# A decoder block on one core: 24 sets of weight sums instead of 20, four FFN blocks with five by-seven steps, and seven by-seven steps in the second half of the down product

## The chip, the cores and the metric

The kernel runs on one core of one Trainium2 chip, in one launch. The metric is the device time of one execution in microseconds (us). Three runs of the kernel before took 1697.29, 1697.33 and 1697.82 us (median 1697.33). The profile comes from one more execution with the hardware profiler on, which took 1698.13 us.

## The reference, cut to what matters

One layer of a hybrid decoder: normalisation, one wide projection, dilated window attention and a gated linear recurrence, a gated merge, the mixing product, and a SwiGLU feed-forward (FFN) part. There are 256 positions, the model width is 2048, and the FFN width is 5632.

```python
a = rmsnorm(h, norm_mix_pre)
q_a, k_a, v_a, q_r, f_r, i_r, g_r, gate_a, gate_r = split_columns(a @ w_in)
...
y = sigmoid(gate_a) * (attn @ w_attn_branch) + sigmoid(gate_r) * (r_out @ w_hgrn_branch)
h = h + rmsnorm(y @ w_mix_out, norm_mix_post)

a = rmsnorm(h, norm_ffn_pre)
gt, up = split(a @ w_ffn_gate_up, [5632])
ff = (silu(gt) * up) @ w_ffn_down
h = h + rmsnorm(ff, norm_ffn_post)
```

The change touches the two FFN products: `a @ w_ffn_gate_up` (2048 to twice 5632) and the product with `w_ffn_down` (5632 to 2048).

## The kernel before, in words

**One product in three matmuls.** Every float32 operand is split into a high and a low part. A product of a weight tile and an activation tile is then three 128x512 matmuls on TensorE (PE): high by high, high by low, low by high (`prod` in `multiply_wide`, all recorded at L138). A weight tile arrives by DMA on SyncE's queue (SP) as `raw`. ScalarE (ACT) copies it to its high part (`w`, `dh`: L418, L426, L429, L439, L442, L445), and VectorE (DVE) subtracts that to get the low part (`wl`, `dl`: L420, L427, L430, L447, L449). PE needs both.

**Wide blocks and steps.** The FFN's gate and up columns are worked in 11 blocks, each a `Wide` of 512 gate and 512 up columns. A block has 8 steps, one for each 256 rows m of the weight, and the order of the steps is written out by hand as a list of pairs (m, code). The down product is two such blocks of 22 steps. A plain step (code 0) is a 2 by 2 product of tiles done with 8 products, 24 matmuls. A "by-seven" step uses a scheme of the kind of Strassen's with 7 products, 21 matmuls. It multiplies sums of weight tiles by sums of activation tiles (`by_sums`, with `w` and `wl` of the sums) and raw tiles by others (`by_raw`, with `dh` and `dl` of the raw weights). With code 1 the sums of the weights are made on DVE when the step is prepared (`sum`, L434, L440, L441). With code 2 they were made long before and are fetched from DRAM (`s`).

**Buffers and the order of work.** While step i multiplies, step i+2 is split (`prepare`, `split_wide`). There are three buffers for `raw`, three for `w`, and four with the tag "d" that `dh` and `dl` share, so that two by-seven steps can hold theirs at once. `by_sums` comes first and `by_raw` second, but in the last by-seven step of a block, and in all of the down product, it is the other way round. Each engine works off its instructions in the order in which this program issues them.

**The list before.** In the FFN, block 0 is plain, block 1 has three by-seven steps (`GATE_UP3`), and blocks 2 to 10 have four (`GATE_UP4`). Two steps of each block 1 to 10 have code 2: 20 sets of weight sums. In the down product the first half has by-seven steps at m = 4, 7, 10, 13, 16, 19, the second at m = 3, 6, 9, 12, 15, 18. For each of these, `prep_act` makes the sums of its activations on DVE (`seven_sums`, L522 to L529) and keeps them in `a7`.

**Weight sums ahead of time.** `weight_sums` is a generator that runs in the background of the 176 narrow items ("chunks") between the wide blocks, in which attention and recurrence are worked too. After each chunk `ahead_of_time` moves it on by one `yield`, unless `hold` is set. For a set it starts two loads of 512 KB into the single buffer `pre` (on SP), lets four items pass, issues two subtractions on DVE (L309, L310), an item later two more (L312, L313), and an item later the store of 1 MB to DRAM (`presum`, on ACT's queue, L316). That is seven items a set. In the same stretch a chunk's weight is split by ACT (L364) and DVE (L365) ahead of the chunk's matmuls, two chunks ahead.

The sums of the activations for the FFN's by-seven steps (`h7`) are made in `pair_sums` out of `hT`, one set for each m, and live in slots of 1024 columns (`rslot`).

Of the kernel before, what the change touches and what calls it, by code (L numbers as in the profile page):

```python
# [24 lines left out]
FF = 5632  # L25
# [17 lines left out]
]  # L43
GATE_UP3 = [(3, 0), (4, 0), (0, 2), (5, 0), (1, 1), (6, 0), (2, 2), (7, 0)]
GATE_UP4 = [(4, 0), (5, 0), (0, 2), (6, 0), (1, 1), (2, 2), (3, 1), (7, 0)]
PLACE = (0, 2, 1, 3)
DOWN = [[(m, m in by7) for m in range(KF // 2)] for by7 in (range(4, 20, 3), range(3, 19, 3))]

N_F, N_RAW, N_SPLIT, AHEAD, WARM, BRIDGE = 15, 3, 3, 2, 8, 6

# [50 lines left out]
def tile_hybrid_block(ctx: ExitStack, tc: tile.TileContext, t, out):  # L101
# [13 lines left out]
    def nm(s):  # L115
        serial[0] += 1
        return f"{s}_{serial[0]}"

    def rslot(s):
        return rpool.tile([P, 1024], F32R, tag="r", bufs=16, name=nm(s))  # L120
# [10 lines left out]
    def p3(s, dtype, n, bufs, tag=None):  # L131
        return wide_pool[-1].tile([P, n], dtype, tag=tag or s, bufs=bufs, name=nm(s))
# [161 lines left out]
    def weight_sums(jobs):  # L294

        for n in jobs:
            x = fp[0].tile([P, 2048], F32, tag="pre", bufs=1, name=nm("pre"))
            b, i = steps[n][:2]
            m = b.order[i][0]
            for g in range(2):  # L300
                nc.sync.dma_start(
                    x[:, g * 1024 : (g + 1) * 1024].rearrange("p (k c) -> p k c", k=2),
                    b.w[2 * m * P : (2 * m + 2) * P, b.cols[g] : b.cols[g] + 512]
                    .rearrange("(k p) c -> p k c", p=P),
                )
            for _ in range(4):
                yield
            r = [x[:, q * 512 : (q + 1) * 512] for q in range(4)]
            nc.vector.tensor_sub(r[2], r[2], r[0])  # L309
            nc.vector.tensor_sub(r[0], r[1], r[0])  # L310
            yield
            nc.vector.tensor_add(r[1], r[1], r[2])  # L312
            nc.vector.tensor_sub(r[3], r[3], r[1])  # L313
            yield
            pre[n] = dram.tile([P, 2048], F32, name=nm("presum"))
            nc.scalar.dma_start(pre[n], x)  # L316
            yield
# [327 lines left out]
        return row[:, None, :].to_broadcast([P, n, S])  # L645

    evacs, turns, lanes, queue = deque(), deque(), [deque(), deque()], deque()
    back, hold = deque(), [False]
    ready = set()

    def advance(q):
# [586 lines left out]
    def mix_to_ffn(i):  # L1238
# [60 lines left out]
        ffn(2, 1)  # L1299
        residual_of(5, (0, 1), False)  # L1300

    def more_h(c):
        if c + 1 < KD // 2:
            transpose_in(h_t, colg[:, 16:32], hT[0], c + 1)
        if c == 3:
            mix_gain(3, 1, wides[last_mix])
            residual_of(6, (0, 1), False)
            residual_of(7, (0, 1), False)
            lanes[0].append(second_norm())
        if c == 4:  # L1310
            lanes[1].append(pair_sums(hT[0], h7, lambda: rslot("so"), range(4)))

    def second_norm():
        ss, s2 = small("ss"), small("s2")
# [86 lines left out]
    def prep_act(m, by7):  # L1401

        q = prepared[0] // 2
        prepared[0] += 1
        fetch_act(q + (m % 2 and 2))
        f = act_in[q][:, m % 2 * 2 : m % 2 * 2 + 2, :]
        x = parts_of[m] = Split("a", 2)
        x.high(0, f)
        yield
        x.low(0, f)  # L1410
        if by7:
            dst = rslot("so").rearrange("p (z n t) -> p z n t", z=2, n=4)
            high, low = seven_sums(f, dst)
            high()
            a7[m] = sums_of(dst)
            yield
            low()
# [154 lines left out]
    add_wide_block(w, (0, FF), PLAIN, lambda k: hT[0](k), None, evac_first, True, mid=more_h)  # L1572
    spare = wides[-1], 0
    for j in range(1, 11):
        add_wide_block(w, (512 * j, FF + 512 * j), GATE_UP4 if j > 1 else GATE_UP3, lambda k: hT[0](k),
                       lambda m: h7[m], evac_ffn, j % 2 == 0,
                       pre=begin_wides if j == 1 else None, turn=1)
    for j in range(2):
# [19 lines left out]
    split(1)  # L1598
    load_upto(AHEAD + N_RAW - 1)
    for i in range(len(items)):  # L1600
        kind, n, _ = items[i]
        b, c = kind[n][:2]
        wide = kind is steps
        if wide:
            now[0] = b
        if c == 0 and b.pre:
            b.pre()
        if not wide and n in items_pre:
            items_pre[n]()
        if together <= i < together + 5:  # L1610
            if i == together:
                flush(evacs)
                mix_to_ffn(i)
            continue
        if not (wide and b.mid):
            prepare(i)
        if i >= len(items) - 3:
            continue
        multiply(i)
        if b.post:  # L1620
            b.post(c)
        if wide and c == b.last7:
            gather(b)
        advance(evacs)
        if wide and c == b.turn:
            flush(evacs)
            turn_act(turns.popleft())
        for _ in range(2):
            if turns and type(turns[0]) is not list:
                advance(turns)  # L1630
        advance_lanes()
        if not wide:
            ahead_of_time()
        if c == (len(b.order) if wide else b.steps) - 1:
            evacs.append(b.evac(b if wide else b.banks))
            if wide:
                advance(evacs)
# [63 lines left out]
```

## Time and profile before

| | |
|---|---|
| median of 3 runs | 1697.33 us |
| lowest, highest | 1697.29, 1697.82 us |
| profiled execution | 1698.13 us |
| its span of instructions | 1696.3 us |
| HBM read, written | 376.92 MB, 35.13 MB |
| matmuls of the group `acc<-w,hT` (the largest of the FFN) | 472, 152.7 us busy |
| DMA for the sums' loads, stores and fetches | 40 of 512 KB, 20 of 1024 KB, 40 of 512 KB |

The span is the time from the first to the last instruction of the core in the profiled execution, and the rest of its time lies around the span. A view by windows gives each engine's busy time in a stretch; a timeline gives one row for an instruction or a run of like ones: its start, its duration, engine, line, operation with output and inputs, and in brackets how long the engine was idle before it and whom it waited for. Matmuls overlap in the rows (a 128x512 matmul has 0.39 us, and the next starts 0.23 us behind it).

### The profile page before, as it was taken

To read this page: it belongs to the slowest core of one execution; us is meant where nothing else is said; L and a number is where in the kernel's file an instruction comes from. 1 tells how busy PE (TensorE), PEld (TensorE's weight loads), DVE (VectorE), ACT (ScalarE), POOL (GpSimd) and SP (SyncE) were. 2 spreads that over 40 slices of the span, in tenths; PEclk is the share of its full clock that TensorE was granted. 3 is DMA by queue.
4 is the path that set the end of the run, shared out by engine and by line. 5 is a ranking of instruction groups with operands and counts; after the bars stand their busy time and mean duration, and the time that the engine had idled before them with its cause. 6 is when DMAs were issued, how large, how long until landed. Compare 5 with 4: busy or idle time off the path is not lost.

```text
span 1696.3 us, 21711 instructions
## 1 busy us (share of the span) xinstructions
PE 1685.2 (99%) x8260; PEld 1416.7 (84%) x8260; DVE 1436.2 (85%) x1662; ACT 914.7 (54%) x1034; POOL 3.9 (0%) x13
## 2 busy tenths in 40 slices
PE   9999999999999999999999999999999999999997
PEld 7888888888888888888888888888888888888886
DVE  6999888867998988885668888888888888898997
ACT  6655555544444434445445547555555555565663
POOL 0000000000000000000000000000000000000000
PEclk9999999999999999999999999999999999999999
DMA  8667666768677767787858646777777777777773
GB/s 285 205 224 243 230 233 228 234 222 309 225 254 252 256 223 243 253 310 275 295 172 275 210 162 227 269 250 252 254 255 253 249 248 272 257 266 256 248 244 130
DMA packets 228904, 413.48 MB, mean 244 GB/s; under 512 B 12816, under 2 KB 79552, under 8 KB 226240
## 3 DMA queue, kind: packets, MB, share of 16 engines
q1 hardware_dynamic: 218544, 373.93, 65.4%
q10 hardware_dynamic: 10192, 38.15, 6.0%
q8 instruction: 64, 1.05, 0.3%
q14 instruction: 40, 0.33, 0.1%
q0 software_dynamic: 64, 0.02, 0.0%
HBM read 376.92 MB, written 35.13 MB: 243 GB/s over the span
## 4 chain that ended last, share of the span: by engine, by line
PE 98%; DVE 1%; ACT 0%; issue 0%; DVEq 0%; ACTq 0%
PE acc L138 62%; PE aux L138 34%; PE aux L930 0%; DVE wl L420 0%; PE aux L610 0%; PE aux L1348 0%; DVE fz L1475 0%; PE acc L1348 0%; ACT w L418 0%; ACT junk L1429 0%; PE aux L597 0%; DVE e L1425 0%; PE aux L1110 0%; DVE yT L578 0%; PE aux L1220 0%
## 5 line engine op out<-in xcount | busy, mean ns | idle before, releaser
L138 PE MATMUL acc<-xT,w 128*128 128x256 f32 (+1 forms) x2048 | 366.8, 338 | 0.0
L420 DVE TENSOR_TENSOR wl<-raw,w 128x2048 fp32r<-128x2048 f32 (+1 forms) x141 | 306.6, 2182 | 68.8 <-ACT w L418 67.1
L138 PEld LDWEIGHTS acc<-xT,w 128*128 128x128 f32 x2048 | 311.9, 188 | 44.7 <-DVE w L365 0.3
L418 ACT ACTIVATE w<-raw 128x2048 fp32r<-128x2048 f32 (+1 forms) x141 | 256.3, 1827 | 109.3 <-PE acc L138 35.1
L364 ACT ACTIVATE w<-raw 128x1024 fp32r<-128x1024 f32 x176 | 185.7, 1058 | 220.5 <-PE acc L138 169.6
L365 DVE TENSOR_TENSOR w<-raw,w 128x1024 fp32r<-128x1024 f32 x176 | 214.8, 1221 | 95.9 <-ACT w L364 95.2
L138 PE MATMUL acc<-w,xT 128*128 128x512 f32 x578 | 169.1, 392 | 0.0
L439 ACT ACTIVATE w<-sum 128x1024 fp32r<-128x1024 f32 x56 | 59.5, 1063 | 177.8 <-DVE sum L434 170.6
L138 PE MATMUL acc<-w,hT 128*128 128x512 f32 x472 | 152.7, 391 | 0.4 <-DVE hT L1232 0.4
L447 DVE TENSOR_TENSOR wl<-sum,w 128x1024 fp32r<-128x1024 f32 x112 | 134.8, 1221 | 13.2 <-ACT w L439 13.2
L138 PEld LDWEIGHTS acc<-w,xT 128*128 128x128 f32 x578 | 108.1, 188 | 22.2
L138 PE MATMUL aux<-w,hT 128*128 128x512 f32 x374 | 120.0, 389 | 0.0
L449 DVE TENSOR_TENSOR dl<-raw,dh 128x1536 fp32r<-128x1536 f32 x56 | 98.3, 1756 | 14.3 <-ACT dh L445 12.2
L138 PE MATMUL aux<-w,xT 128*128 128x512 f32 x344 | 109.8, 389 | 0.0
L138 PEld LDWEIGHTS acc<-w,hT 128*128 128x128 f32 x472 | 88.5, 188 | 19.0 <-DVE hT L1232 0.8
L138 PE MATMUL acc<-wl,hT 128*128 128x512 f32 x236 | 91.9, 389 | 0.0
L445 ACT ACTIVATE dh<-raw 128x1536 fp32r<-128x1536 f32 x56 | 82.7, 1476 | 8.0 <-PE aux L138 4.4
L138 PE MATMUL acc<-w,a 128*128 128x512 f32 x268 | 83.7, 389 | 0.0
L138 PE MATMUL aux<-w,a 128*128 128x512 f32 x268 | 83.7, 389 | 0.0
L138 PEld LDWEIGHTS aux<-w,hT 128*128 128x128 f32 x374 | 70.2, 188 | 14.6
L138 PE MATMUL acc<-w,so 128*128 128x512 f32 x234 | 78.8, 391 | 0.0
L138 PEld LDWEIGHTS aux<-w,xT 128*128 128x128 f32 x344 | 64.6, 188 | 13.4
(298 smaller groups left out, 2964.3 us busy)
## 6 DMA issues: line engine op xcount, KB each, us to landing
raw<-in_w_in SPq DMA_DIRECT2D x270, 512.0 KB, 4.8
raw<-in_w_ffn_gate_up SPq DMA_DIRECT2D x156, 512.0 KB, 4.8
raw<-in_w_ffn_down SPq DMA_DIRECT2D x88, 512.0 KB, 5.4
pre<-in_w_ffn_gate_up SPq DMA_DIRECT2D x40, 512.0 KB, 6.5
presum<-pre ACTq DMA_DIRECT2D x20, 1024.0 KB, 4.7
s<-presum SPq DMA_DIRECT2D x40, 512.0 KB, 7.0
raw<-in_w_mix_out SPq DMA_DIRECT2D x32, 512.0 KB, 4.9
act<-acts SPq DMA_DIRECT2D x22, 512.0 KB, 6.5
```

The costliest lines, as they stand in the source:

```text
L138: nc.tensor.matmul(ps, lhsT, rhs, start=start, stop=stop, skip_group_check=True)
L364: nc.scalar.activation(wh, raw, AF.Copy)
L365: nc.vector.tensor_sub(wl, raw, wh.bitcast(F32))
L418: nc.scalar.activation(hi[:, c], raw[:, c], AF.Copy)
L420: nc.vector.tensor_sub(lo[:, c], raw[:, c], hi[:, c].bitcast(F32))
L439: nc.scalar.activation(hi[:, :1024], s[:, :1024], AF.Copy)
L445: nc.scalar.activation(dhi, d, AF.Copy)
L447: nc.vector.tensor_sub(lo[:, c], s[:, c], hi[:, c].bitcast(F32))
L449: nc.vector.tensor_sub(dlo, d, dhi.bitcast(F32))
```

## The change

There are four edits.

1. `GATE_UP5` is a new list with five by-seven steps, one after the other, and blocks 3, 5, 7 and 9 use it. The step m = 4, plain before, becomes a by-seven step with code 2. This makes 24 sets of weight sums instead of 20.
2. The second half of the down product has by-seven steps at m = 2, 4, 7, 10, 13, 16, 18. Those at 4, 7, 10, 13 and 16 use the activation sums that the first half made (`m not in a7`), so two sets are made in this half instead of six.
3. `weight_sums` starts the loads of a set only behind an odd item (`count[0]`), and three items pass before the first pair of subtractions instead of four. A set takes six items.
4. `pair_sums` makes a fifth set of `h7` (m = 4). Its first four slots come from the tag "so" of the wide blocks' pool, the fifth from `rslot`.

```diff
+GATE_UP5 = [(5, 0), (6, 0), (0, 2), (2, 2), (1, 1), (4, 2), (3, 1), (7, 0)]
 PLACE = (0, 2, 1, 3)
-DOWN = [[(m, m in by7) for m in range(KF // 2)] for by7 in (range(4, 20, 3), range(3, 19, 3))]
+DOWN = [[(m, m in by7) for m in range(KF // 2)] for by7 in (range(4, 20, 3), (2, 4, 7, 10, 13, 16, 18))]
...
         for n in jobs:
+            while count[0] % 2 == 0:
+                yield
             x = fp[0].tile([P, 2048], F32, tag="pre", bufs=1, name=nm("pre"))
...
-            for _ in range(4):
+            for _ in range(3):
                 yield
...
-    back, hold = deque(), [False]
+    back, hold, count = deque(), [False], [0]
...
+    def h7_slot():
+        return p3("so", F32R, 1024, 4) if len(h7) < 4 else rslot("so")
+
...
-            lanes[1].append(pair_sums(hT[0], h7, lambda: rslot("so"), range(4)))
+            lanes[1].append(pair_sums(hT[0], h7, h7_slot, range(5)))
...
-        if by7:
+        if by7 and m not in a7:
             dst = rslot("so").rearrange("p (z n t) -> p z n t", z=2, n=4)
...
-        add_wide_block(w, (512 * j, FF + 512 * j), GATE_UP4 if j > 1 else GATE_UP3, lambda k: hT[0](k),
+        order = GATE_UP3 if j == 1 else GATE_UP5 if j in (3, 5, 7, 9) else GATE_UP4
+        add_wide_block(w, (512 * j, FF + 512 * j), order, lambda k: hT[0](k),
...
-        kind, n, _ = items[i]
+        count[0], (kind, n, _) = i, items[i]
```

The lists and the pacing move instructions on DVE and ACT. Three places follow. The numbers behind the names count tiles, and the line numbers of the changed kernel are up to six higher than before.

**ACT, an FFN block with the new list (block 3), and the block in the same place before.** `L426` and `L429` make `w` and `dh` of a code 2 step, `L439`, `L442` and `L445` those of a code 1 step, `L418` is a plain step, and the rows on `act` hand over the results of the block before. Before, from the step (0,2) to (1,1):

```order
L426 ACTIVATE w_9301<-s_9227 128x1024
L426 ACTIVATE w_9301<-s_9228 128x1024
L429 ACTIVATE dh_9307<-raw_9199 128x1536
L418 ACTIVATE w_9344<-raw_9231 128x2048
L1349 ACTIVATE act_9379<-acc_9380 128x512
L1349 ACTIVATE act_9379<-acc_9386 128x512
L1353 DMA acts_9392<-act_9379 128x1024
L439 ACTIVATE w_9394<-sum_9396 128x1024
L442 ACTIVATE w_9394<-sum_9396 128x1024
L445 ACTIVATE dh_9402<-raw_9268 128x1536
```

And now, from (0,2) to (1,1):

```order
L429 ACTIVATE w_9351<-s_9273 128x1024
L429 ACTIVATE w_9351<-s_9274 128x1024
L432 ACTIVATE dh_9357<-raw_9245 128x1536
L429 ACTIVATE w_9394<-s_9314 128x1024
L429 ACTIVATE w_9394<-s_9315 128x1024
L432 ACTIVATE dh_9400<-raw_9277 128x1536
L1355 ACTIVATE act_9435<-acc_9436 128x512
L1355 ACTIVATE act_9435<-acc_9442 128x512
L1359 DMA acts_9448<-act_9435 128x1024
L442 ACTIVATE w_9450<-sum_9452 128x1024
L445 ACTIVATE w_9450<-sum_9452 128x1024
L448 ACTIVATE dh_9458<-raw_9318 128x1536
```

The plain step (6,0) between the two has given way to the code 2 step (2,2). Behind these rows follow (4,2) and (3,1), where before (2,2) and (3,1) stood, so five steps with a `dh` stand one behind the other.

**DVE, the same two places.** `L427` and `L430` make the low parts of a code 2 step, `L420` that of a plain one, `L434` begins the sums of the weights of a code 1 step, and the rows on `e` work on the results of the block before. Before:

```order
L427 TENSOR_TENSOR wl_9302<-s_9227,w_9301 128x1024
L427 TENSOR_TENSOR wl_9302<-s_9228,w_9301 128x1024
L430 TENSOR_TENSOR dl_9308<-raw_9199,dh_9307 128x1536
L1385 TENSOR_TENSOR e_9255<-e_9255,e_9257 128x512
L1385 TENSOR_TENSOR e_9256<-e_9256,e_9258 128x512
L420 TENSOR_TENSOR wl_9345<-raw_9231,w_9344 128x2048
L434 TENSOR_TENSOR sum_9396<-raw_9268 128x1024
```

And now:

```order
L430 TENSOR_TENSOR wl_9352<-s_9273,w_9351 128x1024
L430 TENSOR_TENSOR wl_9352<-s_9274,w_9351 128x1024
L433 TENSOR_TENSOR dl_9358<-raw_9245,dh_9357 128x1536
L1391 TENSOR_TENSOR e_9301<-e_9301,e_9303 128x512
L1391 TENSOR_TENSOR e_9302<-e_9302,e_9304 128x512
L430 TENSOR_TENSOR wl_9395<-s_9314,w_9394 128x1024
L430 TENSOR_TENSOR wl_9395<-s_9315,w_9394 128x1024
L433 TENSOR_TENSOR dl_9401<-raw_9277,dh_9400 128x1536
L437 TENSOR_TENSOR sum_9452<-raw_9318 128x1024
```

Where one `wl` of 2048 columns stood, two of 1024 and a `dl` of 1536 stand.

**DVE, the recurrence stretch, around chunks 75 to 77.** `w<-raw,w` are the low halves of chunks, `pre` the weight sums, the rest attention. Before:

```order
L365 TENSOR_TENSOR w_4719<-raw_4524,w_4719 128x1024
L884 TENSOR_TENSOR w_4738<-sum_4712,tabs 64x512 x2
L365 TENSOR_TENSOR w_4741<-raw_4575,w_4741 128x1024
L890 TENSOR_TENSOR sum_4712<-sum_4712,tabs 128x512
L891 TENSOR_TENSOR qk_4601<-sum_4712,w_4738 128x512
L309 TENSOR_TENSOR pre_4496<-pre_4496 128x512
L310 TENSOR_TENSOR pre_4496<-pre_4496 128x512
L365 TENSOR_TENSOR w_4770<-raw_4575,w_4770 128x1024
```

And now:

```order
L312 TENSOR_TENSOR pre_4469<-pre_4469 128x512
L313 TENSOR_TENSOR pre_4469<-pre_4469 128x512
L368 TENSOR_TENSOR w_4730<-raw_4533,w_4730 128x1024
L887 TENSOR_TENSOR w_4749<-sum_4721,tabs 64x512 x2
L315 TENSOR_TENSOR pre_4469<-pre_4469 128x512
L316 TENSOR_TENSOR pre_4469<-pre_4469 128x512
L368 TENSOR_TENSOR w_4754<-raw_4584,w_4754 128x1024
L893 TENSOR_TENSOR sum_4721<-sum_4721,tabs 128x512
L894 TENSOR_TENSOR qk_4610<-sum_4721,w_4749 128x512
L368 TENSOR_TENSOR w_4783<-raw_4584,w_4783 128x1024
```

Both pairs of a set have moved ahead of the low halves of chunks 75 and 76, and none stands ahead of chunk 77 any more.

## The prediction, made before the changed kernel ran

> **What bounds the kernel now.** I read the page first: the busy share of TensorE and the chain that ended last.
>
> ```profile
> PE 1685.2 (99%) x8260; PEld 1416.7 (84%) x8260; DVE 1436.2 (85%) x1662; ACT 914.7 (54%) x1034; POOL 3.9 (0%) x13
> ...
> PE 98%; DVE 1%; ACT 0%; issue 0%; DVEq 0%; ACTq 0%
> ```
>
> The matmuls are the time: PE is busy for 1685.2 us of the span, and 98% of the chain is PE. VectorE (DVE) comes next, and its 85% is a mean over stages. The view of PE's waits says what little PE waited for:
>
> ```profile
> PE aux L138 <- DVE warm L162: 1.2, 1, 1.2
> PE acc L138 <- DVE hT L1232: 0.4, 1, 0.4
> PE acc L138 <- DVE gate L1147: 0.2, 1, 0.2
> ```
>
> So a matmul that goes is worth its full place in PE's row, unless a new wait takes the place. The view by windows, cut where the L1348 transposes of successive FFN blocks start, prices one product (three 128x512 matmuls). The first row is a block with three by-seven steps, the second one with four. Columns: window, length, busy time of PE, PEld, DVE, ACT and POOL with counts, granted clock, DMA share, GB/s.
>
> ```profile
> 1048.05:1090.42 42.37, 42.37 (x192) 35.17 (x191) 37.85 (x38) 23.82 (x21) 0.00 (x0) 1.00 0.80 269
> 1090.42:1132.12 41.70, 41.70 (x190) 34.61 (x189) 36.70 (x33) 24.13 (x21) 0.00 (x0) 1.00 0.74 254
> ```
>
> PE is busy without a gap in both, so one product less is 42.37 − 41.70 = 0.67 us. DVE is busy for 36.70 of 41.70 us, with room on the mean only.
>
> **The change, part by part.**
>
> *Removed matmuls.* Four FFN blocks lose one product each, and the down product's second half loses one (seven by-seven steps for six): 5 × 0.67 = 3.35, with matmul starts (below) 5 × 0.68 = 3.40. I take **−3.4 us**. That is 0.20% of 1697.33, just the size below which a measurement of this kernel can't tell a change from none (3.39 us). So even the full gain is at the edge, and any wait pulls it inside.
>
> *FFN blocks 3, 5, 7, 9.* Now five by-seven steps follow one another: s2 = (0,2), s3 = (2,2), s4 = (1,1), s5 = (4,2), s6 = (3,1). Tiles dh and dl share four buffers, which is two steps' worth. So ACT may write dh of a step only when PE has left the step two places back. Before, only the third and fourth in a row had to ask ((2,2) and (3,1)), with a plain step behind. The trace shows this wait at (3,1). The first fence is PE, the second ACT, the third DVE; columns are start, duration, operation, and in brackets the idle time before and its releaser.
>
> ```profile
> 1189.20 0.39 PE L138 MATMUL aux<-dl,hT 128*128 128x512 f32 x1
> ...
> 1194.64 0.39 PE L138 MATMUL acc<-dl,hT 128*128 128x512 f32 x1
> ```
>
> ```profile
> 1176.90 1.05 ACT L442 ACTIVATE w<-sum 128x1024 fp32r<-128x1024 f32 x1
> 1177.85 1.48 ACT L445 ACTIVATE dh<-raw 128x1536 fp32r<-128x1536 f32 x1
> ...
> 1187.68 1.06 ACT L442 ACTIVATE w<-sum 128x1024 fp32r<-128x1024 f32 x1 [0.33 <-DVE sum L441]
> 1189.63 1.49 ACT L445 ACTIVATE dh<-raw 128x1536 fp32r<-128x1536 f32 x1 [0.89 <-PE aux L138]
> ```
>
> ```profile
> 1179.36 1.76 DVE L449 TENSOR_TENSOR dl<-raw,dh 128x1536 fp32r<-128x1536 f32 x1
> ...
> 1183.31 1.75 DVE L430 TENSOR_TENSOR dl<-raw,dh 128x1536 fp32r<-128x1536 f32 x1
> 1184.98 1.22 DVE L434 TENSOR_TENSOR sum<-raw 128x1024 f32<-128x1024 f32 x1
> ...
> 1191.15 1.76 DVE L449 TENSOR_TENSOR dl<-raw,dh 128x1536 fp32r<-128x1536 f32 x1 [1.16 <-ACT dh L445]
> ```
>
> The 20th of the 21 matmuls of (1,1) starts at R = 1189.20 and dh(3,1) at R + 0.43. Its dl ends at 1192.91; PE reads it at 1194.64, 24 matmuls behind R (5.44/24 = 0.2267 each), 1.73 early. In the changed blocks this chain begins one step sooner and is one step longer. From R in s3: dh(s5) at R + 0.43; dl(s5) 1.52 later (1189.63→1191.15); then on DVE's queue, behind it, the sums of s6, 1.67 later (1183.31→1184.98); ACT's second high half 2.70 behind these (1184.98→1187.68); dh(s6) 0.95 behind that (1176.90→1177.85); dl(s6) 1.51 later (1177.85→1179.36), lasting 1.76. Sum: R + 10.54. PE reads dl(s6) as the second matmul of s6, because the last by-seven step of a block takes its raw products first: one matmul left of s3, 21 of s4, 21 of s5, two of s6, so R + 45 × 0.2267 = R + 10.20. **PE waits 0.34 us.** What a short wait for DVE costs beside itself shows at the one PE has now:
>
> ```profile
> 1004.87 0.40 PE L138 MATMUL acc<-wl,hT 128*128 128x512 f32 x1
> 1005.68 0.73 PE L138 MATMUL acc<-w,hT 128*128 128x512 f32 x2 [0.41 <-DVE hT L1232]
> 1006.25 0.39 PE L138 MATMUL acc<-wl,hT 128*128 128x512 f32 x1
> ```
>
> The three steps from 1004.87 to 1006.25 take 1.38 where 0.68 is usual: 0.70 lost for 0.41 of waiting. I take about half of that surplus beside the 0.34: 0.5 us a block, four blocks, **+2.0**. Ends: 0 (the chain 0.34 shorter, 3% of its length) and 0.8 a block (3.2 in all).
>
> *More sets of weight sums (24 for 20), every six items for seven.* They run in the recurrence stretch, where DVE also makes the low half of each weight chunk (L365). A set has two pairs of subtractions, L309/L310 and L312/L313. Four sets add 8 pairs, and nearly all others move to other chunks. Where DVE idles ahead of PE a pair costs nothing; where it runs full it makes the next low half late. The worst place, by the order, is where both pairs of a set now stand ahead of the low halves that before stood at 569.26 and 571.93, with none there before. DVE first, then ACT:
>
> ```profile
> 571.93 1.23 DVE L365 TENSOR_TENSOR w<-raw,w 128x1024 fp32r<-128x1024 f32 x1
> ...
> 574.41 0.68 DVE L309 TENSOR_TENSOR pre<-pre 128x512 f32<-128x512 f32 x1
> 575.12 0.69 DVE L310 TENSOR_TENSOR pre<-pre 128x512 f32<-128x512 f32 x1
> 575.73 1.22 DVE L365 TENSOR_TENSOR w<-raw,w 128x1024 fp32r<-128x1024 f32 x1
> ...
> 614.13 1.23 DVE L365 TENSOR_TENSOR w<-raw,w 128x1024 fp32r<-128x1024 f32 x1
> ```
>
> ```profile
> 574.89 1.06 ACT L364 ACTIVATE w<-raw 128x1024 fp32r<-128x1024 f32 x1 [2.21 <-PE acc L138]
> ...
> 616.84 1.06 ACT L364 ACTIVATE w<-raw 128x1024 fp32r<-128x1024 f32 x1 [2.19 <-PE acc L138]
> ```
>
> A pair takes 575.73 − 574.41 = 1.32. DVE's rows show no idle time for 15 us ahead, so the low half of 571.93 ends at 573.16 + 2.64 = 575.80. ACT's row at 574.89, which waits for PE to leave the chunk before, is when PE wants it: 0.9 late, about 1.0 with restarting. The pairs that stood behind it (574.41 and one more) leave the next chunks, which gives back some 0.3 (chosen between 0 and 1.0). The other place is the chunk of 614.13: its low half ends at 615.36 and is wanted at 616.84, a margin of 1.48. Two pairs make it 2.64 − 1.48 = 1.16 late, of which about 0.6 is lost, as PE itself comes 0.7 later from the first place (1.0 − 0.3). At the other moved pairs I found an idle stretch or a margin. Sum **+1.3**, ends 0 and 6 (each of the four new sets giving 1.5 us).
>
> *Down product, second half.* By-seven steps are m = 2, 4, 7, …; at m = 2 and m = 4 only one plain step lies between, and raw products come first. The high and low parts of m = 4, laid end to end on DVE behind the evacuation:
>
> ```profile
> 1572.58 0.68 DVE L578 TENSOR_TENSOR a<-act,a 128x512 fp32r<-128x512 f32 x1
> ...
> 1576.30 1.22 DVE L434 TENSOR_TENSOR sum<-raw 128x1024 f32<-128x1024 f32 x1
> ...
> 1579.49 0.28 DVE L522 SCALAR_TENSOR_TENSOR s<-act 128x128 f32<-128x128 f32 x1
> ...
> 1580.42 2.35 DVE L447 TENSOR_TENSOR wl<-sum,w 128x1024 fp32r<-128x1024 f32 x2
> 1582.69 0.68 DVE L529 TENSOR_TENSOR so<-s,so 128x512 fp32r<-128x512 f32 x1
> ...
> 1584.96 0.74 DVE L1434 SCALAR_TENSOR_TENSOR fz<-e,r2c,fpost 128x512 f32<-128x512 f32 x1
> ...
> 1589.09 0.68 DVE L578 TENSOR_TENSOR a<-act,a 128x512 fp32r<-128x512 f32 x1
> ```
>
> ```profile
> 1587.82 0.39 PE L138 MATMUL aux<-dl,a 128*128 128x512 f32 x1
> ```
>
> A by-seven step's DVE work is 1584.96 − 1576.30 = 8.66; the piece from 1584.96 to 1589.09 stands for the plain step between, 4.13. The second by-seven step reuses its activation sums, so the 0.93 (1579.49→1580.42) and about 0.6 of L529 fall away: 7.13. From 1572.58: 8.66 + 4.13 + 7.13 = 1592.50. PE reads dl of before's m = 3 at 1587.82; the new m = 4 comes a by-seven step (4.76, 21 matmuls) later, 1592.58. No margin: **+0.2**, ends 0 and 0.6. Four sets of sums fewer shorten nothing else, since DVE is late nowhere else there.
>
> *At no cost:* the fifth set of hT sums falls in block 1, where DVE is busy 37.85 of 42.37 us; five fresh instructions of about 0.3 to 0.7 us would show only if that 4.5 us were gone. Each five-step block reads 768 KB more (768 KB raw and two times 512 KB of sums for 1 MB raw), 19 GB/s over 41 us; with the 254 GB/s shown this is 273, near the 269 (share 0.80) that block 1 bears without a gap.
>
> **Sum:** −3.4 + 2.0 + 1.3 + 0.2 = +0.1. The profiled execution took 1698.13 us (span 1696.3 and 1.8 around it), 0.8 above the median of the three runs; I put the difference to the median: 1697.33 + 0.1 = **1697.4**.
>
> **Rivals.**
>
> *A. The gain is whole.* DVE chains have slack that I do not see: an idle queue would start the sums of s6 before dl(s5), were they ordered so. Against it stands the order in which they are issued; for it, that all three overruns are under 1.2 us. Time 1697.33 − 3.4 = 1693.9.
>
> *B. The sums' round trip binds (slower).* A set has one buffer: load it, four subtractions, store it, and only then load the next. The page's rows of DMA issues end in the median to landing:
>
> ```profile
> pre<-in_w_ffn_gate_up SPq DMA_DIRECT2D x40, 512.0 KB, 6.5
> presum<-pre ACTq DMA_DIRECT2D x20, 1024.0 KB, 4.7
> s<-presum SPq DMA_DIRECT2D x40, 512.0 KB, 7.0
> ```
>
> ```profile
> L309 DVE TENSOR_TENSOR pre<-pre x20: 675/684/692, 366.3 to 827.6; 128x512 f32<-128x512 f32 x20
> ```
>
> ```profile
> DMA to landing us min/median/max: 3.9/6.7/8.7
> ```
>
> The first row is the view of L309, the second that of the tile `presum`, stores and loads together. From issuing the store to the next set's first pair lie the store (4.7) and the load (6.5, its second half some 0.9 behind): 12.1 us. After the change four items lie there, before five. The row of L309 gives a mean item: 19 sets of seven items in 461.3 us, 3.47 each, so 13.9 us for four and 17.3 for five. A plain item without attention or recurrence is eight matmuls of 512 columns and eight of 256, 8 × 1.5 × 0.2267 = 2.72; four of these are 10.9. Where the trip is the longer, DVE stands at L309 for a load, with low halves behind it and PE behind those. With 8.7, the longest landing, for both transfers a trip takes 17.4, which is 3.5 over 13.9; less DVE's margin of about 1.5 it costs PE 2 us. If one set in eight meets that, three sets: 1697.4 + 5.8 = 1703. It decides from trips of 13.9 + 1.5 = 15.4 us on. Against it: medians give 12.1. The Trainium skill, "DMA: Bandwidth & Descriptors", section "Latency and other measured facts", says that HBM's access time is 0.2 us on average and 2 us at high load, and that it makes most of a DMA's fixed cost. It speaks against the shorter cycle, whose two transfers each end in such an access: at two more times 2 us every trip would be 16.1, 0.7 over the 15.4, and 24 sets would give 17 us more, 1714. The trace shows 4.7 for a megabyte stored with that time already in it, so I give this nothing beyond B's chance.
>
> *C. Late in more places.* 40 moved pairs fall on chunks that I hold to have margin. If the two places are really seven, at 0.6 each, that is +3: 1700.4.
>
> **How the numbers follow.** Forecast (gain eaten by short waits, 1695.6 to 1699.5 by the bounds taken together) 0.67; A 0.18, of which 0.13 lies at or past the 0.2% bound; C 0.05; B 0.10. The range from 1693.8 to 1700.8 holds the forecast, most of C and about half of A, 0.80. Faster 0.13; slower B with half of C, 0.12; same 0.75.
>
> **What would show it.** PE's waits should gain four rows' worth of `dl` (L452 in the new numbering) of 0.3 to 0.6 us; windows of the odd blocks should be 41.0 + 0.5. The stretch around 575 and 615 should show PE waiting for the low half. If odd blocks take 41.0 without waits, my chain is wrong by its 0.34 and A holds; if the subtractions of the sums (L312 in the new numbering) sit idle for `pre`, B does. DVE idle for `pre` at many sets, or a gap in an FFN block over 1 us, would break the sum.

## The result, and the profile after

The changed kernel took 1700.83 us (median of 12 runs, 1699.95 to 1703.45), the kernel before beside it 1697.78 us (12 runs, 1697.02 to 1698.13). The ratio is 1.0019, with a 95% interval from 1.0011 to 1.0027: 0.2% slower. That is 0.03 us beyond the upper end of the range on record, 1700.8. Against the kernel before beside it the change is +3.05 us, where the prediction had +0.1. The profiled execution took 1700.86 us, with a span of 1699.1.

The page of the changed kernel answers to the two lines shown of before, and its rows of DMA issues to two of the three of the sums:

```profile
PE 1684.6 (99%) x8245; PEld 1413.2 (83%) x8245; DVE 1453.8 (86%) x1677; ACT 920.9 (54%) x1041; POOL 3.8 (0%) x13
...
PE 90%; DVE 5%; DMA 2%; ACT 1%; issue 1%; SPq 0%; DVEq 0%; ACTq 0%
...
pre<-in_w_ffn_gate_up SPq DMA_DIRECT2D x48, 512.0 KB, 5.7
presum<-pre ACTq DMA_DIRECT2D x24, 1024.0 KB, 6.4
```

PE has its 15 matmuls less, but the chain that ended last now runs for 8% of the span through DVE, DMA and ACT; before it was PE for 98%. At the median a set's store takes 1.7 us longer to land than before (6.4 for 4.7), and a load 0.8 less (5.7 for 6.5). The view of PE's waits names two new ones:

```profile
PE acc L139 <- DVE w L368: 2.1, 4, 0.8
PE aux L139 <- DVE warm L163: 1.2, 1, 1.2
PE aux L139 <- DVE dl L452: 1.0, 4, 0.3
```

`w L368` is the low half of a weight chunk in the recurrence stretch, and `dl L452` that of the step (3,1) in the four odd FFN blocks. The view of DVE's waits shows what DVE itself stood for in the stretch:

```profile
DVE pre L312 <- DMA pre<-in_w_ffn_gate_up: 10.6, 8, 2.9
...
DVE pre L312 <- issue: 3.9, 4, 2.4
```

In 12 of 24 sets DVE stood for the loads of the sums, 14.5 us in all. (Where the second row says `issue`, the pair starts about 0.1 us behind the landing of the set's second load, as it does in the first row.) Before, it was 1.9 us in all, at 3 sets. The windows of an odd and an even block (the odd one is the first row):

```profile
1135.43:1177.04 41.61, 41.35 (x186) 33.98 (x185) 37.88 (x34) 24.37 (x21) 0.00 (x0) 1.00 0.73 242
1093.74:1135.43 41.69, 41.69 (x189) 34.62 (x188) 36.76 (x34) 25.60 (x23) 0.00 (x0) 1.00 0.79 277
```

An odd block is 0.08 us shorter than an even one, where one product less is worth 0.68.

**Where the time went, by stages.** The first matmuls wait for the inputs, and differ by up to a us between executions of any kernel, so the stretch is counted from PE's 101st matmul to the first transposes of the FFN (L1348 before, L1354 after); the rest is from there to PE's last matmul. Both are differences of starts in the trace of one execution. The stretch varies from execution to execution: the runs of the changed kernel spread over 3.5 us, those of the kernel before over 1.1.

| kernel | stretch, us | against before | rest, us | against before |
|---|---|---|---|---|
| before | 1023.02 | | 638.59 | |
| after | 1026.35 | +3.33 | 637.80 | −0.79 |
| new pacing alone | 1029.64 | +6.62 | 638.62 | +0.03 |
| down product alone | 1023.07 | +0.05 | 638.16 | −0.43 |
| after, dl(4,2) later | 1026.56 | +3.54 | 635.42 | −3.17 |
| after, early store | 1025.89 | +2.87 | 637.61 | −0.98 |
| after, buffer in halves | 1030.43 | +7.41 | 637.58 | −1.01 |
| after, one load only | 1024.36 | +1.34 | 637.65 | −0.94 |
| after, tenth set later | 1024.63 | +1.61 | 637.64 | −0.95 |
| 22 sets, seven items | 1030.92 | +7.90 | 636.78 | −1.81 |
| 24 sets, fourth set later, dl(4,2) later | 1023.81 | +0.79 | 635.41 | −3.18 |
| 22 sets, last six at six items | 1029.92 | +6.90 | 636.75 | −1.84 |

So the rest, with the FFN and the down product, gave 0.8 us of the 3.4, and the stretch lost 3.3. PE's matmuls, held against those of before one by one, fall back there in steps: 0.57 at 410 (of the time before) and 0.12 right behind, 0.89 at 427, 0.92 at 575 (0.13 of it won back at 583), 0.42 at 617, 0.24 near 463, and a few of 0.1.

### The profile page after: what moved, and what is told of

It reads as the page before. It is cut to its first block, busy times and chain, and to the rows that moved or that the text cites. A ratio compares the mean times of both kernels' runs of the same rounds, so it can differ in the third digit from the quotient of the medians.

```text
span 1699.1 us, 21740 instructions
## 1 busy us (share of the span) xinstructions
PE 1684.6 (99%) x8245; PEld 1413.2 (83%) x8245; DVE 1453.8 (86%) x1677; ACT 920.9 (54%) x1041; POOL 3.8 (0%) x13
## 4 chain that ended last, share of the span: by engine, by line
PE 90%; DVE 5%; DMA 2%; ACT 1%; issue 1%; SPq 0%; DVEq 0%; ACTq 0%
PE acc L139 57%; PE aux L139 32%; DVE w L368 1%; DMA pre<-in_w_ffn_gate_up 1%; DMA presum<-pre 1%; DVE dl L452 0%; PE aux L933 0%; ACT dh L432 0%; DVE wl L423 0%; ACT dh L448 0%; PE aux L613 0%; PE aux L1354 0%; DVE fz L1481 0%; DVE sum L437 0%; PE acc L1354 0%
## 5 line engine op out<-in xcount | busy, mean ns | idle before, releaser
L423 DVE TENSOR_TENSOR wl<-raw,w 128x2048 fp32r<-128x2048 f32 (+1 forms) x136 | 295.4, 2179 | 64.5 <-ACT w L421 62.6
L421 ACT ACTIVATE w<-raw 128x2048 fp32r<-128x2048 f32 (+1 forms) x136 | 246.8, 1823 | 98.3 <-PE acc L139 31.1
L368 DVE TENSOR_TENSOR w<-raw,w 128x1024 fp32r<-128x1024 f32 x176 | 214.5, 1221 | 76.6 <-ACT w L367 74.3
L442 ACT ACTIVATE w<-sum 128x1024 fp32r<-128x1024 f32 x57 | 60.6, 1063 | 182.2 <-DVE sum L437 176.6
L452 DVE TENSOR_TENSOR dl<-raw,dh 128x1536 fp32r<-128x1536 f32 x57 | 100.2, 1757 | 15.6 <-ACT dh L448 13.9
L139 PE MATMUL aux<-w,hT 128*128 128x512 f32 x318 | 102.8, 389 | 0.0
L139 PE MATMUL acc<-w,so 128*128 128x512 f32 x264 | 88.9, 391 | 0.0
L139 PE MATMUL aux<-w,a 128*128 128x512 f32 x254 | 79.4, 389 | 0.0
L139 PE MATMUL acc<-wl,xT 128*128 128x512 f32 x193 | 75.1, 389 | 0.0
```

The source lines that it names most:

```text
L139: nc.tensor.matmul(ps, lhsT, rhs, start=start, stop=stop, skip_group_check=True)
L368: nc.vector.tensor_sub(wl, raw, wh.bitcast(F32))
L421: nc.scalar.activation(hi[:, c], raw[:, c], AF.Copy)
L423: nc.vector.tensor_sub(lo[:, c], raw[:, c], hi[:, c].bitcast(F32))
L442: nc.scalar.activation(hi[:, :1024], s[:, :1024], AF.Copy)
L452: nc.vector.tensor_sub(dlo, d, dhi.bitcast(F32))
```

## The experiments

**1 and 2: two parts alone.** The first kernel has the pacing alone, with the old lists and 20 sets.

```diff
+            while count[0] % 2 == 0:
+                yield
             x = fp[0].tile([P, 2048], F32, tag="pre", bufs=1, name=nm("pre"))
...
-            for _ in range(4):
+            for _ in range(3):
```

> The kernel before with the new pacing of the weight sums alone (six items a set, loads behind odd items; still 20 sets, the old lists of steps). Theory: nearly all of the loss ahead of the FFN comes of the pacing, not of the four extra sets, so the first FFN block's transposes start about 3.2 us later than in the kernel before (1051.2 for 1048.05) and the whole is 1701.0 (+3.2). Rival (the four extra sets load it): the transposes stay within 0.8 us of 1048.05 and the whole within 1 us of the kernel before.

Measured: 1702.15 us (9 runs, 1700.38 to 1704.42), ratio 1.0024 (1.0014 to 1.0034). The pacing makes the whole loss of the stretch, with no set more than before. The size was missed: +4.4 instead of +3.2. Its profiled execution, the slowest of its runs, shows the same steps at 410, 427, 575 and 617, 0.46 at 421, and some 3 us between 460 and 465, where the changed kernel lost 0.24. These 3 us follow the fifth set's load. It took 8.8 us to land here and 7.4 in the changed kernel, and DVE stood 2.35 us for it instead of 1.00. DVE's and PE's timelines:

```profile
456.51 0.69 DVE L311 TENSOR_TENSOR pre<-pre 128x512 f32<-128x512 f32 x1 [2.35 <-issue]
```

```profile
463.00 2.00 PE L138 MATMUL aux<-q,kk 128*128 128x64 f32 x16 [0.52 <-DVE q L1042]
```

Behind this wait PE had another of 0.51 us, and its clock fell for a while (last section). The changed kernel shows no wait at either place. So the spread is part of the effect.

The second has the new second half of the down product alone.

```diff
-for by7 in (range(4, 20, 3), range(3, 19, 3))]
+for by7 in (range(4, 20, 3), (2, 4, 7, 10, 13, 16, 18))]
...
-        if by7:
+        if by7 and m not in a7:
             dst = rslot("so").rearrange("p (z n t) -> p z n t", z=2, n=4)
```

> The kernel before with the new second half of the down product alone. Theory: one product less, 0.68, and a wait of some 0.2 for the low part of m = 4, so -0.5 us (1697.3). Rival: the end of the kernel takes it back (its last evacuation or output sets the end), 0 us (1697.8).

Measured: 1697.17 us against 1697.74, ratio 0.9997 (0.9988 to 1.0006), which by itself can't be told from none. In the trace the rest is 0.43 shorter, near the 0.48 by which the changed kernel's last part was shorter.

**3: the wait in the odd blocks.** In the changed kernel, DVE's subtraction for dl of the step (4,2) moves behind the sums of (3,1).

```diff
             nc.scalar.activation(dhi, d, AF.Copy)
-            nc.vector.tensor_sub(dlo, d, dhi.bitcast(F32))
+            if m == 4:
+                late.append((dlo, d, dhi))
+            else:
+                nc.vector.tensor_sub(dlo, d, dhi.bitcast(F32))
...
         nc.scalar.activation(hi[:, 1024:], s[:, 1024:], AF.Copy)
         next(prep, None)
+        if late:
+            x, y, z = late.pop()
+            nc.vector.tensor_sub(x, y, z.bitcast(F32))
```

> The changed kernel, in which DVE makes the low part dl of the step (4,2) behind the sums of the weights of (3,1) instead of ahead of them. Theory: the wait of an odd block comes of the chain dh(4,2), dl(4,2), sums of (3,1), and with the sums ahead of the dl it goes: odd blocks take 41.01 instead of 41.61 us, the whole is 2.4 lower than the changed kernel, 1698.4. Rival (DVE has too much work in these blocks, whatever its order): odd blocks stay at 41.5 to 41.7, and the whole at 1700.8.

Measured: 1699.31 us (11 runs, 1697.88 to 1701.1), 1.5 below the changed kernel instead of 2.4; in the trace the rest is 2.38 shorter than the changed kernel's, as expected. Why the medians lie just 1.5 apart is not shown: the profiled execution was the lowest of its runs, 3.0 below the changed kernel's. The window of the same odd block in this kernel:

```profile
1134.83:1175.84 41.01, 41.01 (x186) 34.07 (x185) 37.19 (x34) 24.48 (x21) 0.00 (x0) 1.00 0.72 243
```

It took 41.01 us with PE busy throughout, as did each of the four, and DVE made the same instructions. The order of that work was the cause, not its amount.

**4 and 5: two attempts to shorten the trip** of the single buffer, from the store of a set over the next load to its first pair. In the fourth kernel the store goes out on GpSimd's queue, behind the last subtraction, and its item is left as a pause.

```diff
             nc.vector.tensor_sub(r[3], r[3], r[1])
+            pre[n] = dram.tile([P, 2048], F32, name=nm("presum"))
+            nc.gpsimd.dma_start(pre[n], x)
             yield
-            pre[n] = dram.tile([P, 2048], F32, name=nm("presum"))
-            nc.scalar.dma_start(pre[n], x)
             yield
```

> The changed kernel, in which the store of a set of sums goes out on GpSimd's queue right behind its last subtraction, one item earlier and not through ACT; the pairs of subtractions stand where they did. Theory: the stalls near 410 and 427 us (1.6 us with what follows) come of the trip store, load, pair, and go; those near 575 and 617 (0.9 and 0.4) come of where the pairs stand, and stay: the first FFN transposes start at 1049.5 to 1049.8 instead of 1051.3, and the whole is 1699.1 with less spread. Rival (the places of the pairs alone): 1051.3 and 1700.8 as now.

Measured: 1700.72 us (11 runs), as the changed kernel. It tells less than it was meant to, because most stores did not leave earlier. In the changed kernel ACT mostly stands at the store until the last subtraction is done: the store starts 0.03 us behind it in 20 of 24 sets, and in this kernel 0.3 to 0.5 behind. At the third set, whose store the fourth set's load waits for, it did leave sooner (0.3 us behind the last subtraction instead of 2.6), but it took 7.9 us to land instead of 5.7, and DVE stood 2.3 us at the fourth set as before (2.1). DVE's waits for the loads were no fewer, 16.2 us in all.

In the fifth, `pre` is in three tiles of 512 KB; the first half of a set loads without waiting for a store. One slot of the recurrence's 15 makes room.

```diff
-            x = fp[0].tile([P, 2048], F32, tag="pre", bufs=1, name=nm("pre"))
+            x = [fp[0].tile([P, 1024], F32, tag="pre", bufs=3, name=nm("pre")) for _ in range(2)]
...
-            nc.scalar.dma_start(pre[n], x)
+            for g in range(2):
+                nc.scalar.dma_start(pre[n][:, g * 1024 : (g + 1) * 1024], x[g])
```

> The changed kernel with the buffer of the sums in three halves of 512 KB instead of one of 1 MB (a set's first half is loaded without waiting for the store of the set before, its second half waits for half a store); one of the 15 slots of the recurrence goes to make room. The pairs stand where they did. Theory (the trip from store to load to pair costs the 1.6 us near 410 and 427): DVE's waits for pre, 10.6 us in 8 places, fall below 4, these two steps go, those near 575 and 617 stay, and the whole is 1699.2. Rival (the pairs are late there of themselves): the waits fall, the steps stay, 1700.8.

Measured: 1705.01 us (5 runs), ratio 1.0042 (1.0029 to 1.0055): 4 us worse than the changed kernel. DVE's waits for the loads rose to 18.2 us instead of falling under 4. The third set's second half was issued 2.0 us earlier than in the changed kernel (0.7 of it because PE started that much earlier), but it took 8.0 us to land instead of 5.8, so the first pair, which needs both halves, did not come sooner (401.56 and 401.42). So neither attempt took the trip away, and neither tells the theories apart. Whether the slot that went cost something was not tried alone.

**6: no loads.** Only the first set is loaded; the others work on what the buffer holds.

```diff
+        x = None
         for n in jobs:
...
+            if x is None:
                 x = fp[0].tile([P, 2048], F32, tag="pre", bufs=1, name=nm("pre"))
```

> The changed kernel in which only the first set is loaded, and all later sets work on what the buffer holds (the sums of the weights, and so the output, are not the reference's); the subtractions and stores stay. Theory: no wait of DVE for pre after the first, the steps near 410 and 427 (0.7 and 0.9) gone, 575 and 617 left (0.9 and 0.4), the first FFN transposes 1.2 to 1.7 later than in the kernel before instead of 3.3, the whole 1699.1, and its runs no more spread than those of the kernel before (1.5 us; the changed kernel: 3.5). Rival (places of the pairs alone): 3.3 later, 1700.8.

Measured: 1698.15 us (11 runs, 1697.55 to 1698.82), 2.7 below the changed kernel, and with a spread of 1.3 us where it has 3.5. The stretch is 1.34 longer than before. The steps left are 0.88 at 575 and 0.40 at 617, with some of 0.12 each way; that at 427, which the runs 1, 3, 4, 5 and 7 have at 0.8 to 0.9, is gone, and that at 410 too. The step at 410 isn't in the runs 4 and 7 either, and it goes with DVE's stand at the third set: 2.1 to 2.4 us in the changed kernel and the runs 1, 3 and 9, which have it at 0.6 to 0.7, but 1.8 and 1.5 us in the runs 4 and 7, and none here. PE's waits in this kernel:

```profile
PE aux L139 <- DVE dl L454: 1.0, 4, 0.3
PE acc L139 <- DVE w L370: 1.0, 2, 0.7
```

The pairs stand where they did, and two waits for a low half are left of four. The kernel also loads 23 times 1 MB less, so by itself it can't tell the trip from the traffic of the loads; the ninth run keeps the loads.

**7: the tenth set's pairs two items later.**

```diff
-            for _ in range(3):
+            for _ in range(5 if n == jobs[9] else 3):
                 yield
```

> The changed kernel with the tenth set's pairs of subtractions two items later, ahead of the chunks 77 and 78, where the kernel before had its pairs; all later sets follow two items later too. Theory (a pair ahead of a full DVE costs PE): the steps near 575 (0.92, then -0.13) and 617 (0.42) go, and the whole is 1699.6, unless a pair further on falls on another full place. Rival (DVE has 2.64 us more work in the stretch, whatever the place): the loss comes a few chunks later, 1700.8.

Measured: 1699.69 us (11 runs). The steps at 575 and 617 are gone, and the loss does not come back later: the stretch is 1.61 longer than before, where the changed kernel's is 3.33. The step of 0.91 at 427 stays. About 0.7 of the difference between the two traces is the step at 410, which lies ahead of the tenth set and is not of this edit; the rest, and the 1.1 us between the medians, is what was expected of the places of the pairs.

**8 and 10: the old pacing with 22 sets.** Blocks 3 and 5 have five by-seven steps, and dl(4,2) is made later as in the third run. The pacing of the eighth is the one of before; in the tenth the last six sets have six items, without the wait for an odd item.

```diff
-            while count[0] % 2 == 0:
-                yield
...
-            for _ in range(3):
+            for _ in range(4):
                 yield
```

> The changed kernel with the old pacing (seven items a set), which leaves room for 22 sets, so that only the blocks 3 and 5 have five by-seven steps, and with the low part of (4,2) made behind the sums of (3,1). Theory: the stretch of the recurrence is as long as before (two more sets cost 0 to 0.5), the two blocks save 0.68 each and the down product 0.5, so 1695.9 to 1696.4, below the kernel before (1697.7). Rival (five by-seven steps and their sums cost as much as they save, whatever the pacing): 1697.2.

Measured: 1704.33 us (5 runs), ratio 1.0044 (1.0031 to 1.0057). Up to 870 us the stretch is no longer than before. There the 22nd set is flushed at the end of the stretch, both pairs at once and with the load just issued. The timelines of DVE and of PE:

```profile
870.66 0.69 DVE L310 TENSOR_TENSOR pre<-pre 128x512 f32<-128x512 f32 x1 [6.41 <-DMA pre<-in_w_ffn_gate_up]
```

```profile
875.10 0.79 PE L139 MATMUL acc<-w,attnT 128*128 128x512 f32 x1 [5.10 <-ACT w L365]
```

DVE stands for the load, ACT's queue stands at the store behind it, and PE loses some 7.8 us, by which the expectation was missed. The FFN gave its 1.36 and the down product its 0.45, so the rival (the steps cost what they save) does not hold either. The tenth run was to remove the flush:

```diff
-            for _ in range(4):
+            for _ in range(3 if n in jobs[16:] else 4):
                 yield
```

> As the eighth run (22 sets, blocks 3 and 5, low part of (4,2) later), with six items for seven in the last six sets only, from chunk 126 on, so that the last set ends in time and isn't flushed at the end of the stretch. Theory: the one stall of the eighth run (7.9 us near 870) came of this flush and goes; the stretch is as long as before to 0.5 us, the FFN saves 1.36, the down product 0.5: 1695.9 to 1696.6. Rival: six items are too short there too, and a stall of a us or more shows behind 770: 1697.5 or more.

Measured: 1702.25 us (7 runs), ratio 1.0026 (1.0015 to 1.0038). The rival was right. The flush is gone, but from the 18th set on DVE stands 4.7 to 6.8 us for every load, and PE falls back by 4.7 us from 823 on and by 2 more behind 846. The case of the 19th set is in SP's timeline of this kernel, and under it is that of the changed kernel:

```profile
786.86 6.92 SPq L270 DMA_DIRECT2D raw<-in_w_hgrn_branch  x4
793.88 0.93 SPq L302 DMA_DIRECT2D pre<-in_w_ffn_gate_up  x2
```

```profile
766.10 0.88 SPq L304 DMA_DIRECT2D pre<-in_w_ffn_gate_up  x2
767.21 14.12 SPq L270 DMA_DIRECT2D raw<-in_w_in  x6
```

Without the wait for an odd item these sets fall on the other items. The load then stands on SP behind the loads of a chunk pair, which wait for a buffer: it goes out at 793.88, 3.0 us after the store has landed (790.89), and all of it has landed 7.7 later (801.55). Behind an odd item it goes out as the store lands (766.10 and 766.08), ahead of the next chunk loads, and has landed 6.1 later (772.22). In the five sets the load went out 0.0, 3.0, 3.9, 1.0 and 2.8 us after the store had landed, and took 7.6 to 10.8 us; the changed kernel's last five went out within 0.1 and took 5.0 to 6.1. So the wait for an odd item does shorten the trip, though for the 18th set, which went out at once, the queue was not the cause.

**9: 24 sets, the fourth set's pairs two items later, dl(4,2) later.**

```diff
-            for _ in range(3):
+            for _ in range(5 if n == jobs[3] else 3):
                 yield
```

> The changed kernel with two more items between load and pairs of the fourth set (its pairs then stand ahead of the chunks 35 and 36 instead of 27 and 34, and all later pairs two chunks later, so the tenth set's at 77 and 78), and with the low part of (4,2) behind the sums of (3,1). Theory: the FFN gives 4 times 0.6 as in the third run; the step near 427 (0.9), where DVE stood for this set's load, goes, and those near 575 and 617 go as in the seventh run; what is left is the step near 410 and a few tenths elsewhere. Whole 1696.4 to 1697.0, spread still 2 us or more because six items are hardly longer than the trip. Rival (each trip is late anyway, and the wait only moves to the next set): 1698.3.

Measured: 1695.57 us (11 runs, 1694.99 to 1697.51) against 1697.55 of the kernel before, ratio 0.9990 (0.9982 to 0.9999). It is faster than both kernels, by 2.0 us against the one beside it and by about 5 against the changed one, and 0.8 better than the lower end expected. Of the waits for a low half, one is left, and PE's dl is not among the waits:

```profile
PE acc L139 <- DVE w L368: 0.4, 1, 0.4
```

All loads are made, DVE still stands 12.6 us for them in 9 sets, and the stretch is just 0.79 longer than before. So neither the traffic of the loads nor the sum of DVE's waits makes the loss by itself; what counts is at which chunk DVE stands.

## Why the prediction was wrong, point by point

**What bounds the kernel, and the 3.4 us:** right. The steps that lost a product got shorter by 0.68 each wherever no wait took the place (third run: 4 × 0.68 + 0.43 = 3.15, measured 3.17).

**The FFN blocks, +2.0:** right in mechanism, close in size. A block lost 41.61 − 41.01 = 0.60 instead of 0.5, in all 2.4. The chain is in the timeline of the changed kernel as it was added up. ACT first, then DVE, then PE:

```profile
1145.81 1.49 ACT L432 ACTIVATE dh<-raw 128x1536 fp32r<-128x1536 f32 x1 [1.38 <-PE acc L139]
```

```profile
1147.34 1.76 DVE L433 TENSOR_TENSOR dl<-raw,dh 128x1536 fp32r<-128x1536 f32 x1 [0.73 <-ACT dh L432]
1149.01 1.22 DVE L437 TENSOR_TENSOR sum<-raw 128x1024 f32<-128x1024 f32 x1
...
1154.19 1.76 DVE L452 TENSOR_TENSOR dl<-raw,dh 128x1536 fp32r<-128x1536 f32 x1 [0.15 <-ACT dh L448]
```

```profile
1156.01 0.50 PE L139 MATMUL aux<-dl,hT 128*128 128x512 f32 x1 [0.26 <-DVE dl L452]
```

From dh(4,2) at 1145.81 to the end of dl(3,1) at 1154.19 + 1.76 = 1155.95 it is 10.14 us; the prediction had 10.54 − 0.43 = 10.11. What was short is what a wait costs beside itself: PE waits 0.26 by the row and loses 0.60.

**The down product, −0.68 + 0.2:** right, −0.43 alone.

**The pairs of subtractions, +1.3:** the two places are right (0.92 − 0.13 + 0.42 = 1.21; 1.34 for the stretch without the loads). What failed is the sentence that ends that step, "At the other moved pairs I found an idle stretch or a margin", and with it the sum of +1.3, where the stretch lost 3.33. The margins were worked out as if the weights were always in the buffer when DVE came to them. They were not, and the stretch lost some 2.0 us more than without the loads; between the medians of the changed kernel and the sixth run it is 2.7.

**Rival B** had that mechanism, with a chance of 0.10, and was priced as one case apart: 1703, from trips of 15.4 us on. The sign that the prediction gave for a broken sum, DVE idle for `pre` at many sets, is what the trace shows.

Three things were off in it. The medians of the landings gave a trip of 12.1 us. Taken set by set, from the issue of a store to the landing of both loads behind it, the median was 13.7 us before and 13.1 in the changed kernel (11.3 to 16.2), so the trip did not grow. Against it stood a mean item, 4 × 3.47 = 13.9 us, and the mean hides short ones. At the third and fourth sets the trips took an ordinary 12.2 and 11.3 us, far from the 15.4, but DVE came to the pair 10.0 and 9.4 us after the store had gone out, less than four plain items, 4 × 2.72 = 10.9.

The whole round of the second set, from one load's issue to the next, took 18.3 us (376.87 to 395.14: load 7.6, subtractions and the low halves between them 4.6, store 6.0), where six plain items are 6 × 2.72 = 16.3. And the margin is not 1.5 us at every set. A stand of 2.06 us at the fourth set cost 0.9 and one of 1.00 at the fifth 0.24, but one of 2.94 at the 19th and one of 2.15 at the 23rd cost PE nothing. At the third set, where DVE stood 2.4 us, the stand went on through an evacuation to ACT and on to PE. The timeline of DVE there:

```profile
401.42 0.69 DVE L312 TENSOR_TENSOR pre<-pre 128x512 f32<-128x512 f32 x1 [2.37 <-issue]
402.15 0.69 DVE L313 TENSOR_TENSOR pre<-pre 128x512 f32<-128x512 f32 x1
402.76 1.22 DVE L368 TENSOR_TENSOR w<-raw,w 128x1024 fp32r<-128x1024 f32 x1
403.89 0.68 DVE L315 TENSOR_TENSOR pre<-pre 128x512 f32<-128x512 f32 x1
404.61 0.69 DVE L316 TENSOR_TENSOR pre<-pre 128x512 f32<-128x512 f32 x1
...
407.14 0.69 DVE L800 TENSOR_TENSOR q<-sum,rowb 128x512 f32<-128x512 f32 x1
...
409.48 1.22 DVE L368 TENSOR_TENSOR w<-raw,w 128x1024 fp32r<-128x1024 f32 x1 [1.65 <-ACT w L367]
```

ACT's, in the same stretch:

```profile
407.86 0.63 ACT L801 ACTIVATE sig<-q 128x512 f32<-128x512 f32 x1 [4.48 <-DVE q L800]
407.92 0.33 ACTq L319 DMA_DIRECT2D presum<-pre  x1
408.40 2.94 ACT L367 ACTIVATE w<-raw 128x1024 fp32r<-128x1024 f32 x3
```

And the two waits of PE that follow from this set and the next:

```profile
410.75 17.10 PE L139 MATMUL acc<-xT,w 128*128 128x256 f32 x96 [0.42 <-DVE w L368]
428.49 0.73 PE L139 MATMUL acc<-xT,w 128*128 128x256 f32 x3 [0.64 <-DVE w L368]
```

`q` (L800) follows the pairs on DVE's queue, ACT's work on `sig` needs it, and the store and ACT's next high halves stand behind that work; DVE's row at 409.48 waits for one of them. A margin of DVE's low halves alone does not see this path.

**HBM's access time**, which the prediction took from the Trainium skill ("DMA: Bandwidth & Descriptors", section "Latency and other measured facts"), was left without weight, and its 1714 was not reached. The page ties this time to the memory that a transfer ends in, which is HBM for the store alone. Counted once it gives 12.1 + 2 = 14.1 us, an estimate, under the 15.4. In the trace the same store of 1 MB took 3.8 to 10.4 us to land in one execution, and no run shows why.

**Not settled:** why the pacing alone, with fewer sets, lost 1.3 us more at the median than the changed kernel, and by which transfers a run is at 1700 or at 1703. The first run's trace shows one such place, the fifth set, where a load that landed 1.4 us later made some 3 us. The fifth run lost 1.8 us at the same place, with a stand of 2.46. The spread goes where the loads go (sixth run), but what makes one load land later than another no run shows.

## What to carry to other kernels

A background job with one buffer has a cycle time of its own, made of its load, its work, its store and the queues that it stands in; compare it, place by place, with the time that the pacing leaves it at the shortest items, before counting its instructions. A mean of both hides the few places where the engine that stands has the next engine behind it. Where a transfer stands on a shared queue (behind a load whose buffer isn't free, or ahead of it) added 3 us and more to a trip here. When an in-order engine makes both a late thing and an early one, the order can matter more than the amount: one subtraction issued behind three others gave back all of the four blocks' waits.

## What the runs showed of the hardware

After PE's idle time at the flush of the eighth run, its granted clock fell. The windows of that kernel:

```profile
865.00:870.00 5.00, 5.00 (x23) 3.80 (x21) 0.00 (x0) 0.00 (x0) 0.00 (x0) 1.00 0.84 309
870.00:875.00 5.00, 0.00 (x1) 0.00 (x0) 2.77 (x4) 1.01 (x2) 0.00 (x0) 0.76 0.13 54
875.00:880.00 5.00, 4.43 (x11) 3.19 (x12) 4.89 (x6) 1.94 (x3) 0.00 (x0) 0.56 0.84 277
```

The third column from the end is the clock: 1.00, then 0.76 and 0.56, while the wait itself was 5.1 us. For some matmuls afterwards each one starts 0.43 us behind the last instead of 0.23, which made about a fifth of the 7.8 us.

In the changed kernel waits of up to 0.8 us left no such mark: the clock was 1.00 in the windows around them. In the first run two waits of half a microsecond, at 463.00 and 465.79, did come ahead of a fall:

```profile
465.00:470.00 5.00, 4.49 (x16) 3.67 (x16) 4.96 (x8) 2.55 (x4) 0.00 (x0) 0.66 0.61 228
```

Up to 469.3 matmuls of 512 columns start 0.43 us apart there, which is about half of the 3 us lost at that place. In the fifth run waits of 0.74 and 0.52 us at the same place left the clock at 1.00. In the tenth run the clock was 0.66 from 825 to 830, behind a wait of 2.8 us, and some 1.6 of the 4.7 us lost there came of it. So a stall can cost more than its wait; how short a stall is harmless the runs do not show.
